# One gated DeltaNet layer on one Trainium2 core: a list scheduler in the source orders all five engines

## Chip, cores, metric

One NeuronCore of a Trainium2 chip. The metric is the device time of one execution in microseconds.

## What is computed

With DEPTH = 1 only the gated DeltaNet layer runs: T = 1024 tokens, D = 1024, 8 query/key heads and 16 value heads of width 128, chunks of 64 tokens in the reference. All of it is float32.

```python
hdn = rms_norm(x, norm_g) * (1 + scale) + shift          # shift, scale, gate from silu(c) @ ada_w
proj = hdn @ w_in                                        # q, k, v (convolved), z, b, a
qkv = silu(causal_depthwise_conv(qkv, conv_w))           # 4 taps
beta = sigmoid(b); g = -exp(a_log) * softplus(a + dt_bias); gc = cumsum(g) in a chunk
A = strict_lower(beta * k k^T * decay);  T = (I + A)^-1
# per chunk, with the state S carried on:
v_new = T (beta v) - T (beta k exp(gc)) S
o = q exp(gc) S + lower(q k^T decay) v_new
S = S exp(g_last) + (k exp(g_last - gc))^T v_new
y = (rms_norm(o) * silu(z)) @ w_out
out = rms_norm(x + gate * y)
```

## The kernel before

The kernel works in chunks of 128 tokens and in groups of two value heads that share one key/query head: 8 groups. Every float32 product of the projections is made of three float32r products (high and low parts of both sides), so one projection tile of 128 channels by 512 tokens is 24 matmuls of 512 columns (`project`, L453).

After a prologue (normalization, modulation, first projections) the main loop (L928) runs nine stages, gi = -1 to 7. In stage gi these generators run side by side:

- `scan` (L677) of group gi: per chunk three matmuls in turn, with VectorE's r (L739), vd (L758) and st (L771) between them, then the output, its norm and its gate z.
- `stage_a` (L534) of group gi+1: `norms` (L487) loads the decay table em from DRAM, exponentiates it, transposes k and q and takes their norms; then 8 products k k^T and q k^T, a store D1 of the diagonal 32x32 blocks and a load ua of them, 62 dependent VectorE operations on tm and tb (L575, L577: the solve), a store D2, and `levels` (L587), which loads TT and puts the 32x32 inverses together to 64 and 128 on TensorE.
- the filler: z projections (`out_gate`, L667), v projections (`values`, L632) of group gi+1, k/q projections (`proj_kq`, L474) of group gi+2. Each half tile of k, q or v goes through `Conv` (L430): two ScalarE copies out of PSUM, three VectorE operations, a SiLU.
- in stage 1 also `residual_gate` (L781).

`load_w` (L130) loads a projection weight tile in two halves (DMA, ScalarE cast, GpSimd subtraction). `early` (L861) begins the output product with the first four of 16 row blocks of w_out, for two time tiles of 512 tokens; it takes the memory of hdn and so can start only after the last projection. It loads w_out's two column halves in turn (`load_wo`, L805) and loads the first again for the second time tile, 12 loads in all.

Only TensorE's order is written out by hand there. `drive` (L902) keeps a clock of its own, `now`, that grows by a cost per matmul; a generator yields (cost, delay) and comes back no sooner than `delay` later. The delays are the constants D_... at L40 to L45, D_L0 = 46000 ns between the last product of `stage_a` and `levels` among them. In between filler matmuls are placed; in the last two stages also the units of `early` (tail), beside the NE = 15 units put into stage 6. The other four engines' instructions are put in order by the framework's scheduler.

After the loop, the other 12 row blocks of w_out follow (`load_wo2`, L814), then the residual, the final norm and the stores.

Of the kernel before, what the change touches and what calls it, by code (L numbers as in the profile page):

```python
# [35 lines left out]
TURN = 40  # L36
MM = 216

START, START1 = 11000, 65000
D_G, D_RG = 9500, 11000  # L40
D_N, D_A0, D_A = 3000, 1500, 1000
D_L0, D_L1, D_L2, D_L3 = 46000, 1600, 1800, 1600
D_R, D_V, D_S = 500, 1100, 700
D_F0, D_F = 8000, 2000
# [3 lines left out]
def gdn_layer(ctx: ExitStack, tc: tile.TileContext, x, c, ada_w, ada_b, norm_g, w_in, conv_w, a_log, dt_bias,  # L48
# [222 lines left out]
    def gates():  # L271

        w4 = lambda name: wpool.tile([P, 4, P], F32, name=name, tag="wraw", bufs=3)
        ba = [w4("ba").rearrange("p a b -> p (a b)") for _ in range(NHALF)]
        gt = w4("gt")
        yv, u, sv, s2 = [gt[:, i] for i in range(4)]
# [5 lines left out]
        pba = q0.tile([P, NT, 2 * HV], F32, name="pba", tag="xn", bufs=1)  # L282
        nc.scalar.copy(pba, ptb[:, :, 2 * HV:])
        nc.vector.tensor_tensor(pba, pba, ptb[:, :, :2 * HV], op=ALU.add)
        gt = w4("gt")
        q, g, grow, below = [gt[:, i] for i in range(4)]
        gh = w4("gh")[:, 0]
        nc.gpsimd.tensor_tensor(below, ones, triu, op=ALU.subtract)
        nc.vector.tensor_tensor(v3(yv), pba[:, :, HV:], dtb[:, None, :].to_broadcast(GS), op=ALU.add)
        nc.scalar.activation(u, yv, AF.Abs)  # L290
        nc.scalar.activation(u, u, AF.Exp, scale=-1.0)
        nc.scalar.activation(beta, pba[:, :, 0:HV], AF.Exp, scale=-1.0)

        nc.vector.tensor_scalar_add(sv, u, 2.0)
        nc.vector.reciprocal(sv, sv)
        nc.vector.tensor_tensor(sv, sv, u, op=ALU.mult)
        nc.vector.tensor_tensor(s2, sv, sv, op=ALU.mult)
        nc.vector.tensor_scalar_mul(q, s2, 1.0 / 17.0)
        for d in (15, 13, 11, 9, 7, 5, 3):
            nc.vector.scalar_tensor_tensor(q, q, 1.0 / d, s2, op0=ALU.add, op1=ALU.mult)  # L300
        nc.vector.scalar_tensor_tensor(q, q, 1.0, sv, op0=ALU.add, op1=ALU.mult)
        nc.vector.tensor_scalar_max(yv, yv, 0.0)
        nc.vector.scalar_tensor_tensor(yv, q, 2.0, yv, op0=ALU.mult, op1=ALU.add)
        nc.vector.scalar_tensor_tensor(v3(g), v3(yv), -1.0, nea[:, None, :].to_broadcast(GS), op0=ALU.mult,
                                       op1=ALU.mult)
        yield 0, D_G

        pgc = bank("ts", (P, 4, P))
        nc.vector.tensor_copy(gh.rearrange("p (h n) -> p n h", n=NT), v3(g))
# [4 lines left out]
        nc.scalar.copy(grow, pgc[:, 3])  # L314
        nc.sync.dma_start(out=gc_dram.rearrange("h n c -> (h n) c"), in_=grow)
        nc.vector.tensor_scalar_mul(ngc, v3(pgc[:, 0]), -1.0)
        nc.scalar.activation(eall, pgc[:, 0:3], AF.Exp)
        nc.vector.tensor_scalar_mul(negc, egc, -1.0)
        nc.vector.tensor_scalar_add(beta, beta, 1.0)
        nc.vector.reciprocal(beta, beta)  # L320
        yield 650, 0
# [94 lines left out]
    gate_steps = gates()  # L416
    with tc.manual_schedule(engines=GENG):
        next(gate_steps)
        drain(len(units))
# [9 lines left out]

    class Conv:  # L430
# [5 lines left out]
        def __call__(self, ps, dst, tag="xb", bufs=2):  # L436
            xb = cp.tile([P, TH + NTAP - 1], F32, name="xb", tag=tag, bufs=bufs)
            if self.prev is None:
                nc.gpsimd.memset(xb[:, 0:NTAP - 1], 0.0)  # L439
            else:  # L440
                nc.vector.tensor_copy(xb[:, 0:NTAP - 1], self.prev[:, TH:])
            nc.scalar.copy(xb[:, NTAP - 1:], ps)
            tp = taps[:, :, self.ct:self.ct + 1]
            nc.scalar.mul(dst, ps, tp[:, NTAP - 1])  # L444
            for j in range(NTAP - 1):
                nc.vector.scalar_tensor_tensor(dst, xb[:, j:j + TH], tp[:, j], dst, op0=ALU.mult, op1=ALU.add)  # L446
            nc.scalar.activation(dst, dst, AF.Silu)
            self.prev = xb
# [4 lines left out]
    def project(w, m, half):  # L453

        ps = bank("pj")
        hi, lo = w
        for k in range(KT):
            for n, (a, b) in enumerate(((hi, h_hi), (hi, h_lo), (lo, h_hi))):
                nc.tensor.matmul(ps[:m], lhsT=a[:, k, :m], rhs=b[half][k // 4][:, k % 4], start=(k == 0 and n == 0),  # L459
                                 stop=(k == KT - 1 and n == 2))  # L460
                yield MM
        return ps

    def trans():
        return bank("tr", (P, 4, P))

    kq0 = new_kq()
    for j, ct in ((0, 8), (1, 0)):
        cv = Conv(ct)
        for hf in range(NHALF):  # L470
            cv(acc0[j][hf], kq0[hf][:, j], tag="vtok", bufs=3)


    def proj_kq(gi, kq):  # L474
        for j, ct in ((0, 8 + gi), (1, gi)):
            w = load_w(ct * P, P, wpool)
            cv = Conv(ct)
            for hf in range(NHALF):
                if j == 0:
                    kq.append(cp.tile([P, 2, TH], F32, name="kq", tag="kq", bufs=4))  # L480
                ps = yield from project(w, P, hf)
                cv(ps, kq[hf][:, j])

    class Group:
        pass

    def norms(gi, G):  # L487

        kq, h0 = G.kq, 2 * gi
        G.em, G.ktok, G.rinv, G.oeps, G.brk, G.bkd, G.TT = [], [], [], [], [], [], []  # L490

        em = cp.tile([P, 2, NT, P], F32, name="em", tag="em", bufs=2)
        nc.sync.dma_start(out=em.rearrange("p h n c -> p (h n c)"),
                          in_=gc_dram[h0:h0 + 2].rearrange("h n c -> (h n c)")[None, :].to_broadcast([P, 2 * T]))
        for n in range(NT):
            for h in range(2):
                nc.vector.scalar_tensor_tensor(em[:, h, n], em[:, h, n], ngc[:, n, h0 + h:h0 + h + 1], mask,  # L497
                                               op0=ALU.add, op1=ALU.add)
        nc.scalar.activation(em, em, AF.Exp)
        for hf in range(NHALF):  # L500
            n0 = 4 * hf

            ssk = cp.tile([P, 4], F32, name="ssk", tag="ssk")
            ssq = cp.tile([P, 4], F32, name="ssq", tag="ssq")
            ktok = cp.tile([P, 4, P], F32, name="ktok", tag="ktok", bufs=4)
            pk = trans()
            for j in range(4):
                nc.tensor.transpose(pk[:, j], kq[hf][:, 0, j * P:(j + 1) * P], ident)
            yield 430, 0
            nc.scalar.copy(ktok, pk)  # L510
            for j in range(4):
                nc.scalar.activation(pk[:, j], pk[:, j], AF.Square, accum_out=ssk[:, j:j + 1])
            pq = trans()
            for j in range(4):
# [19 lines left out]
    def stage_a(gi, G):  # L534

        kq, ats = G.kq, []
        if not hasattr(G, "bkd"):
            yield from norms(gi, G)
# [497 lines left out]
```

## Time and profile before

| | us |
|---|---|
| median of 3 runs | 1133.0 (1131.27 to 1133.68) |
| the profiled execution | 1130.95 |
| its span, first to last instruction | 1129.2 |
| TensorE's mean granted clock | 0.979 of 2.4 GHz |

The rows below come from the page of the profiled execution and from questions to its trace. Engines: PE is TensorE, PEld its weight loads, DVE VectorE, ACT ScalarE, POOL GpSimd, SP the queue that issues DMAs. A group row has line, engine, operation, output<-inputs, shapes and count, then the busy time in us and the mean of one in ns, then the idle time ahead of them and what ended it. A row of stretches has the stretch, its length, per engine the busy time and count, the granted TensorE clock, the share of time the DMA engines worked, GB/s. A row of the time line has start, duration, engine, line, operation. A matmul's duration overlaps the next one's, so the rate of matmuls is read from the distance of their starts.

### The profile page before, as it was taken

The numbers are of one execution on the slowest core, as the hardware profiler recorded it, in microseconds if no ns is written. First come the engines' busy times: TensorE is split into PE (matmuls) and PEld (weight loads), VectorE is DVE, ScalarE is ACT, GpSimd is POOL, SyncE is SP. The second block draws the span as 40 slices with busy tenths as digits, with TensorE's granted clock in tenths as the row PEclk, the third lists the DMA queues.
The fourth block names the chain that finished last, engine by engine and source line by source line (L and its number), as shares of the span: only waits on it lengthen the run. The fifth ranks groups of instructions, "written<-read, shape, count | busy, mean of one in ns | idle before, by whom it ended". The sixth has DMA issues, their size and how long they took to land.

```text
span 1129.2 us, 18338 instructions
## 1 busy us (share of the span) xinstructions
PE 1059.3 (94%) x6295; PEld 857.6 (76%) x6295; DVE 745.1 (66%) x1914; ACT 536.6 (48%) x1416; POOL 450.0 (40%) x532
## 2 busy tenths in 40 slices
PE   8997999989999799999999999999899989999997
PEld 7875787767878678777877887788678768778785
DVE  5468775776579857865786677677766866513515
ACT  6567442453642455435543644364546424534523
POOL 3452223532444135323532452155216334954643
PEclk9998999999999999999999999999999989999999
DMA  9803333341145313421531143125313571446442
GB/s 287 234 19 133 75 82 85 101 126 43 39 135 164 83 50 100 125 56 30 145 102 45 42 146 84 39 54 163 74 29 103 149 219 63 140 135 185 152 121 75
DMA packets 188131, 119.48 MB, mean 106 GB/s; under 512 B 59733, under 2 KB 166534, under 8 KB 187014
## 3 DMA queue, kind: packets, MB, share of 16 engines
q1 hardware_dynamic: 187536, 118.20, 37.2%
q8 instruction: 50, 0.82, 0.3%
q14 instruction: 43, 0.35, 0.1%
q10 hardware_dynamic: 502, 0.10, 0.0%
HBM read 93.03 MB, written 25.24 MB: 105 GB/s over the span
## 4 chain that ended last, share of the span: by engine, by line
PE 41%; DVE 18%; ACT 6%; POOL 5%; DMA 4%; issue 4%; SPq 0%; POOLq 0%; DVEq 0%; ACTq 0%
PE pj L459 16%; PE pj L837 5%; DVE tb L577 4%; DVE tm L575 4%; DVE vT L446 3%; DVE em L497 3%; PE tr L549 2%; PE tr L837 2%; PE ts L755 2%; PE ks L736 1%; PE oq L709 1%; PE oq L762 1%; PE tr L622 1%; PE ks L767 1%; PE tr L628 1%
## 5 line engine op out<-in xcount | busy, mean ns | idle before, releaser
L124 POOL TENSOR_TENSOR wlo<-wraw,whi 128x512 fp32r<-128x512 f32 x92 | 126.1, 1379 | 147.3 <-ACT whi L123 107.7
L446 DVE SCALAR_TENSOR_TENSOR vT<-xb,taps,vT 128x512 f32<-128x512 f32 x96 | 84.6, 882 | 24.3 <-ACT vT L444 23.3
L446 DVE SCALAR_TENSOR_TENSOR kq<-xb,taps,kq 128x512 f32<-128x512 f32 x96 | 78.7, 828 | 12.9 <-ACT kq L444 11.0
L123 ACT CAST whi<-wraw 128x512 fp32r<-128x512 f32 x92 | 55.5, 618 | 64.9 <-PE pj L459 59.0
L577 DVE TENSOR_TENSOR tb<-tb,tm 128x126 f32<-128x126 f32 (+22 forms) x248 | 80.1, 323 | 4.8
L698 POOL TENSOR_TENSOR oT<-oT,z 128x256 f32<-128x256 f32 x64 | 50.6, 792 | 81.2 <-ACT oT L697 74.0
L575 DVE TENSOR_TENSOR tm<-tb,ua 128x126 f32<-128x126 f32 (+22 forms) x248 | 78.3, 316 | 6.2 <-DMA ua<-D 1.1
L459 PE MATMUL pj<-h1hia,whi 128*128 128x512 f32 x184 | 75.8, 412 | 6.6 <-ACT vT L444 6.6
L697 ACT ACTIVATE oT<-pot,cols 128x256 f32<-128x256 f32 x64 | 30.4, 474 | 108.1 <-PE pot L695 54.8
L459 PE MATMUL pj<-h0lob,whi 128*128 128x512 f32 x184 | 78.2, 425 | 0.0
L459 PE MATMUL pj<-h0hia,whi 128*128 128x512 f32 x184 | 76.8, 417 | 1.3 <-ACT kq L444 1.3
L459 PE MATMUL pj<-h1hib,whi 128*128 128x512 f32 x184 | 77.8, 423 | 0.0
L459 PE MATMUL pj<-h1lob,whi 128*128 128x512 f32 x184 | 77.7, 422 | 0.0
L459 PE MATMUL pj<-h1hia,wlo 128*128 128x512 f32 x184 | 77.5, 421 | 0.0
L459 PE MATMUL pj<-h0hib,wlo 128*128 128x512 f32 x184 | 77.1, 419 | 0.0
L459 PE MATMUL pj<-h1hib,wlo 128*128 128x512 f32 x184 | 76.6, 416 | 0.0
L459 PE MATMUL pj<-h0hia,wlo 128*128 128x512 f32 x184 | 75.8, 412 | 0.0
L459 PE MATMUL pj<-h1loa,whi 128*128 128x512 f32 x184 | 75.7, 411 | 0.0
L459 PE MATMUL pj<-h0loa,whi 128*128 128x512 f32 x184 | 75.6, 411 | 0.0
L459 PE MATMUL pj<-h0hib,whi 128*128 128x512 f32 x184 | 75.5, 410 | 0.0
L439 POOL MEMSET xb<- 128x3 f32 x32 | 3.4, 109 | 172.3 <-DVE kq L446 85.9
L719 POOL TENSOR_TENSOR sso<-sso,neg_half 128x2 f32<-128x2 f32 x64 | 44.6, 696 | 58.3 <-DVE sso L718 57.6
(445 smaller groups left out, 2933.1 us busy)
## 6 DMA issues: line engine op xcount, KB each, us to landing
wraw<-in_gdn_w_in SPq DMA_DIRECT2D x92, 256.0 KB, 2.9
woraw<-in_gdn_w_out SPq DMA_DIRECT2D x54, 256.0 KB, 3.2
wa<-in_ada_w SPq DMA_DIRECT2D x16, 512.0 KB, 6.9
em<-gc_dram SPq DMA_DIRECT2D x8, 1024.0 KB, 6.4
z_dram<-sz SPq DMA_DIRECT2D x32, 256.0 KB, 2.1
z<-z_dram SPq DMA_DIRECT2D x64, 128.0 KB, 2.4
o_dram<-oT SPq DMA_DIRECT2D x64, 128.0 KB, 1.9
gsrc<-o_dram SPq DMA_DIRECT2D x32, 256.0 KB, 2.9
```

The lines of the kernel that those rows point to most:

```text
L123: nc.scalar.copy(hi, raw)
L124: nc.gpsimd.tensor_tensor(lo, raw, hi.bitcast(F32), op=ALU.subtract)
L446: nc.vector.scalar_tensor_tensor(dst, xb[:, j:j + TH], tp[:, j], dst, op0=ALU.mult, op1=ALU.add)
L459: nc.tensor.matmul(ps[:m], lhsT=a[:, k, :m], rhs=b[half][k // 4][:, k % 4], start=(k == 0 and n == 0), stop=(k == KT - 1 and n == 2))
L497: nc.vector.scalar_tensor_tensor(em[:, h, n], em[:, h, n], ngc[:, n, h0 + h:h0 + h + 1], mask, op0=ALU.add, op1=ALU.add)
L549: nc.tensor.matmul(pg2[:, 0:2], lhsT=kq[hf][:, 0, js], rhs=kq[hf][:, :, js], start=True, stop=True)
L575: nc.vector.tensor_tensor(tmv, tb[:, :mm, j:j + 1].to_broadcast([P, mm, ln]), ua[:, j:j + 1, j + 1:].to_broadcast([P, mm, ln]), op=ALU.mult)
L577: nc.vector.tensor_tensor(tb[:, :mm, j + 1:], tb[:, :mm, j + 1:], tmv, op=ALU.subtract)
L697: nc.scalar.mul(oT, pot, normw_c)
L698: nc.gpsimd.tensor_tensor(oT, oT, zs.pop(n), op=ALU.mult)
L719: nc.gpsimd.tensor_tensor(sso, sso, neg_half[:, :2], op=ALU.pow)
L837: nc.tensor.matmul(acc, lhsT=a[:, ts], rhs=b, start=(first and n == 0), stop=(last and n == 2))
```

## The change

A class `Order` in the source keeps a model of four queues (ScalarE, VectorE, GpSimd, SP) with a price for each operation. A generator no longer issues an instruction of these engines itself: it puts it into a queue as an `Op` with its price, the operations it must come after and a rank. `advance` takes, as the model's clock reaches them, the operation that can start first, among those of one time the lowest rank, and issues it. A step of TensorE yields a condition (inputs done in the model plus LATP) and is issued at the first moment at which it holds; `drive` asks the streams in a fixed order, the filler last. The whole region is fixed for all five engines. A `loader` runs as a generator of its own through the list of all projection weight tiles. Gates, norms, convolutions, the solve, the levels and the scan compute what they did. `early_loads` keeps both column halves of the first four row blocks of w_out (one in the memory of hdn, one in the projection weights' buffers), so 8 loads. The units of `early` in stage 6 are those that `take` gives; the rest runs in the last stage.

```diff
-TURN = 40
-MM = 216
-START, START1 = 11000, 65000
-D_G, D_RG = 9500, 11000
-D_L0, D_L1, D_L2, D_L3 = 46000, 1600, 1800, 1600
...
+MM, M4, M2, TP = 231, 430, 218, 436
+LAT, LATP, DMA = 150, 250, 2800
+TABLE = 1283
+AC = {512: 530, 256: 400, 128: 240}
+VC = {512: 690, 256: 340, 128: 265}
...
+    def advance(self, upto):
+        while True:
+            best = None
+            for eng, q in self.queue.items():
+                if not q:
+                    continue
+                free = self.free.get(eng, 0)
+                ready = [(max(t, free), op) for op in q[:80] if (t := op.start()) is not None]
+                if not ready:
+                    continue
+                t = min(r[0] for r in ready)
+                op = min((r for r in ready if r[0] <= t), key=lambda r: r[1].rank)[1]
+                if best is None or t < best[0]:
+                    best = (t, eng, op)
+            if best is None or best[0] > upto:
+                return
+            t, eng, op = best
+            self.queue[eng].remove(op)
+            op.fn()
+            if op.table and op.table != self.table:
+                t, self.table = t + TABLE, op.table
+            op.end = t + op.cost
...
+    def loader():
+        while True:
+            yield lambda: bool(wq) and order.avail("w", 2)
+            c0 = wq.pop(0)
...
+                d = load(lambda raw=raw, ks=ks, c0=c0: nc.sync.dma_start(out=raw, in_=wv[:, ks, c0:c0 + P]))
+                a = act(lambda raw=raw, ks=ks, hi=hi: nc.scalar.copy(hi[:, ks], raw), 512, d, rank=2)
+                ops.append(pool(lambda raw=raw, ks=ks, hi=hi, lo=lo: nc.gpsimd.tensor_tensor(
+                    lo[:, ks], raw, hi[:, ks].bitcast(F32), op=ALU.subtract), 1290, a, holds=r))
...
     def norms(gi, G):
...
+        yield lambda: hasattr(order, "gate") and done(*order.gate, order.gc)
+        d = load(lambda: nc.sync.dma_start(
+            out=em.rearrange("p h n c -> p (h n c)"),
...
+        d = order.put("sp", 2500, lambda: None, (d,))
+        e = [vec(lambda n=n, h=h: nc.vector.scalar_tensor_tensor(
+            em[:, h, n], em[:, h, n], ngc[:, n, h0 + h:h0 + h + 1], mask, op0=ALU.add, op1=ALU.add), 128, d, rank=2)
+             for n in range(NT) for h in range(2)]
+        G.emop = act(lambda: nc.scalar.activation(em, em, AF.Exp), 1820, *e, table="exp")
...
     def gates(ptb, held):
+        gt = cp.tile([P, 8, P], F32, name="gt", tag="at", bufs=2)
...
     def stage_a(gi, G, old):
...
+            d = [vec(lambda j=j, mm=mm, ln=ln, tmv=tmv: nc.vector.tensor_tensor(
+                tmv, tb[:, :mm, j:j + 1].to_broadcast([P, mm, ln]), ua[:, j:j + 1, j + 1:].to_broadcast([P, mm, ln]),
+                op=ALU.mult), 170 + mm * ln * 3 // 4, *d, rank=2)]
...
-        yield 0, D_L0
-        yield from levels(gi, G, 0)
+        yield from levels(gi, G, 0, old)
...
     def scan(gi, G):
...
+                ro = [vec(lambda h=h, n=n, pks=pks, r=r, vtok=vtok, j=j: nc.vector.scalar_tensor_tensor(
+                    r[:, h], pks[:, 0, h], negc[:, n, h0 + h:h0 + h + 1], vtok[:, j, h], op0=ALU.mult, op1=ALU.add), 128,
+                          rank=-1) for h in range(2)]
...
+    def early_loads():
+        yield lambda: not order.projecting
...
+            if tg == 0:
+                wset[0] = wos[:EARLY]
+                for i in range(EARLY // 2):
+                    hi, lo = [wpool.tile([P, 2, TH], F32R, name=n, tag=t, bufs=2)
+                              for n, t in (("wohi", "whi"), ("wolo", "wlo"))]
+                    wset[1] += [(hi[:, n], lo[:, n]) for n in range(2)]
...
+            for kt in range(EARLY):
+                yield lambda: order.avail("sz", 2)
+                g(kt, tg)
...
+    def drive(runs, must):
+        idle = 0
+        while not all(r.over for r in must):
+            order.advance(order.now)
+            if any(r.step() for r in runs):
+                idle = 0
             else:
+                order.now += 50
...
-    with tc.manual_schedule(engines={nc.tensor.engine}):
+    with tc.manual_schedule(engines=ORDERED(nc)):
...
+                    more = itertools.chain(done_projecting(), take(tail, NE))
...
+            drive(background + must + ([trun] if gi == HQ - 1 else []), must)
+        drive(background + [trun], [trun])
+        order.flush()
```

## Rows read from the trace of the kernel before

**Rows 1.** The page, section 1: busy us, share of the span, instructions.
```profile
PE 1059.3 (94%) x6295; PEld 857.6 (76%) x6295; DVE 745.1 (66%) x1914; ACT 536.6 (48%) x1416; POOL 450.0 (40%) x532
```

**Rows 2.** Busy time by stretch: stages A, G0, G1, G3, G5, G6, G7, O.
```profile
77.20:183.65 106.45, 98.34 (x537) 78.22 (x537) 80.80 (x219) 56.62 (x135) 29.11 (x35) 0.95 0.35 97
183.65:296.15 112.50, 106.58 (x698) 86.01 (x699) 77.13 (x195) 45.96 (x115) 35.52 (x48) 0.97 0.29 77
296.15:411.34 115.19, 105.96 (x668) 85.81 (x667) 92.30 (x274) 53.51 (x153) 40.48 (x51) 0.99 0.39 106
...
520.46:628.71 108.25, 103.49 (x651) 83.56 (x650) 75.75 (x203) 52.97 (x152) 40.21 (x51) 0.98 0.31 81
...
735.20:841.72 106.52, 101.78 (x651) 82.48 (x650) 75.63 (x203) 53.05 (x152) 39.71 (x51) 1.00 0.31 82
841.72:939.19 97.47, 89.84 (x539) 72.38 (x537) 72.06 (x189) 45.21 (x143) 43.10 (x49) 0.96 0.50 148
939.19:990.00 50.81, 49.12 (x301) 40.55 (x302) 28.77 (x63) 26.63 (x86) 38.06 (x44) 1.00 0.32 98
990.00:1129.20 139.20, 129.00 (x559) 104.06 (x557) 48.96 (x69) 52.46 (x103) 68.99 (x56) 0.99 0.43 135
```

**Rows 3.** Time line of PE: projection matmuls at two moments.
```profile
98.77 0.63 PE L459 MATMUL pj<-h0hib,whi 128*128 128x512 f32 x1
99.20 0.63 PE L459 MATMUL pj<-h0lob,whi 128*128 128x512 f32 x1
...
586.62 0.40 PE L459 MATMUL pj<-h1loa,whi 128*128 128x512 f32 x1
586.85 0.40 PE L459 MATMUL pj<-h1hia,wlo 128*128 128x512 f32 x1
```

**Rows 4.** Waits of PE in G3 (520 to 628): us in total, times, longest.
```profile
PE pj L459 <- ACT vT L444: 1.7, 1, 1.7
PE tr L639 <- ACT vT L447: 0.9, 1, 0.9
PE tr L613 <- ACT pn L609: 0.8, 1, 0.8
PE tr L614 <- DVE pn L610: 0.7, 1, 0.7
PE tr L508 <- ACT tr L512: 0.7, 1, 0.7
```

**Rows 5.** The page, section 6: DMA issues, KB each, median us to landing.
```profile
woraw<-in_gdn_w_out SPq DMA_DIRECT2D x54, 256.0 KB, 3.2
em<-gc_dram SPq DMA_DIRECT2D x8, 1024.0 KB, 6.4
...
ua<-D SPq DMA_DIRECT2D x16, 256.0 KB, 4.1
```

**Rows 6.** Groups of VectorE instructions over the whole span.
```profile
L446 DVE SCALAR_TENSOR_TENSOR kq<-xb,taps,kq 128x512 f32<-128x512 f32 x96 | 78.7, 828 | 12.9 <-ACT kq L444 11.0
...
L497 DVE SCALAR_TENSOR_TENSOR em<-em,ngc,mask 128x128 f32<-128x128 f32 x128 | 50.0, 409 | 1.0 <-DMA em<-gc_dram 1.0
```

**Rows 7.** Waits of PE in G6 and G7 (841 to 990).
```profile
PE pj L837 <- ACT h0hia L810: 3.4, 2, 2.6
PE pj L837 <- DVE h0hib L811: 2.4, 2, 2.1
PE pj L837 <- POOL h0hib L811: 1.0, 1, 1.0
```

**Rows 8.** G6 again, output products (L837) alone: PE, PEld, clock, DMA.
```profile
841.72:939.19 97.47, 27.68 (x96) 18.94 (x96) 0.96 0.50 148
```

**Rows 9.** Time line of DVE and POOL near 567 us.
```profile
566.72 0.30 DVE L575 TENSOR_TENSOR tm<-tb,ua 128x136 f32<-128x136 f32 x1
567.05 1.35 DVE L577 TENSOR_TENSOR tb<-tb,tm 128x136 f32<-128x136 f32 x1
...
566.95 2.60 POOL L124 TENSOR_TENSOR wlo<-wraw,whi 128x512 fp32r<-128x512 f32 x2 [1.41 <-ACT whi L123]
```

More of the change, by code (lines that the diff above doesn't have):

```diff
@@ L457, in project @@
+    def project(c0, half, last):
+        yield lambda: c0 in wready and done(*wready[c0][1]) and free("pj")
+        (hi, lo), _, held = wready[c0]
+        ps, ph = bank("pj"), order.hold("pj", 1 if c0 >= Z0 else 2)
         for k in range(KT):
             for n, (a, b) in enumerate(((hi, h_hi), (hi, h_lo), (lo, h_hi))):
-                nc.tensor.matmul(ps[:m], lhsT=a[:, k, :m], rhs=b[half][k // 4][:, k % 4], start=(k == 0 and n == 0),
+                nc.tensor.matmul(ps, lhsT=a[:, k], rhs=b[half][k // 4][:, k % 4], start=(k == 0 and n == 0),
@@ L460, in project @@
                                  stop=(k == KT - 1 and n == 2))
[L461 to L474, printed above, removed]
+                order.now += MM
+                if k < KT - 1 or n < 2:
+                    yield None
+        if last:
+            held.append(order.mark())
@@ L479, in proj_kq @@
                 if j == 0:
[L480 to L485, printed above, removed]
+                    G.kq.append(cp.tile([P, 2, TH], F32, name="kq", tag="kq", bufs=4))
+                ps, ph = yield from project(ct * P, hf, hf == NHALF - 1)
+                G.kqop[hf][j] = cv(ps, ph, G.kq[hf][:, j], [old.passed[hf]] if old else [])
+                yield None
@@ new lines, in values @@
+        waiting = []
+        source = itertools.chain(tiles(), more or [])
+        end = object()
+        y = next(source, end)
+        while y is not end:
+            if ready():
+                turn(*waiting.pop(0)[1:])
+                yield None
+            elif y is None:
+                yield None
+                y = next(source, end)
+            else:
+                yield lambda: y() or ready()
+                if y():
+                    y = next(source, end)
+        while waiting:
+            yield ready
+            turn(*waiting.pop(0)[1:])
+            yield None
@@ new lines, in gdn_layer @@
+    order.projecting, order.early0 = True, False
+    Gs = [Group(gi) for gi in range(HQ)]
+    zgates = [out_gate(head, Gs[head // 2]) for head in range(HV)]
+    zheads = list(range(HV))
+    background = [Run(loader()), Run(early_loads())]
+    tail = early()
+    trun = Run(tail)
+    rows = []
+    for gi in range(-1, HQ):
+        heads, zheads = zheads[:ZQ[gi + 1]], zheads[ZQ[gi + 1]:]
+        tiles = [16 + 2 * (gi + 1) + h for h in range(2)] if gi + 1 < HQ else []
+        pair = [8 + gi + 2, gi + 2] if gi + 2 < HQ else []
+        zc = [Z0 + h * P for h in heads]
+        wq += ([c * P for c in pair + tiles] + zc) if gi < 0 else zc + [c * P for c in tiles + pair]
```

731 lines of the change are left out of this document (452 added, 279 removed).

## The prediction

> **What bounds the kernel now.** I read the page's line of busy shares first: TensorE is busy for 94% of the span, no other engine for more than 66% [rows 1]. So a change that keeps every matmul can win only what TensorE does not use. To see where that is, the second view cuts the span into stages: a lead-in from the first projection to the first scan (77.20 to 183.65), then one stage per head group, each beginning with the first matmul of its scan, then the output tail from 990 [rows 2]. I call them A, G0 to G7 and O. In each row the reader takes span minus TensorE's busy time, and the granted clock. Idle: A 8.1, G0 5.9, G1 9.2, G2 5.2 and G3 4.8 (one row stands for both), G4 and G5 4.7 each (likewise), G6 7.6, G7 1.7, O 10.2 us. The clock has two levels, so a mean of 0.95 over 106.45 us stands for a tenth of it at 1.2 GHz, and half of that tenth is lost: 0.05 x 106.45 = 5.3 us in A, likewise 3.4 in G0, 1.2 in G1, 2.2 in G2, 2.2 in G3, nothing in G4 and G5, 3.9 in G6. That such stretches exist is seen in matmul starts: 0.43 us apart after the idle time ahead of 98 us, 0.23 us apart elsewhere [rows 3]. Idle plus half-rate loss is 42.6 + 14.3 = 57.0 us in A to G5 and 13.2 in G6 and G7.
>
> Third, who ends the idle time. One ordinary stage, G3, has five waits: 1.7 us for a PSUM bank that ScalarE had not emptied, 0.9 for a SiLU ahead of a transposition, 0.8 and 0.7 in the block inverse, 0.7 for squares, 4.8 in all [rows 4]. No wait for projection weights is among them. So weights do not bound the steady stages, and a stream of their own cannot win there by itself. VectorE's 75.75 us in G3's 108.25 leave it room on average [rows 2].
>
> **The change, part by part.** The sum is made against the profiled execution, 1130.95 us (its span is 1129.2); the median of the three runs is 2.05 us above it.
>
> *Order of TensorE.* Before, a step was placed a fixed delay after the step it depends on; now it is placed when the scheduler's own model says that its inputs are finished plus 0.25 us, and projection matmuls go in wherever nothing else is ready. A perfect model would take all 57.0 us of A to G5: the matmuls themselves are the same, and G5 shows that with 4.7 us of idle time the clock stays at its upper level, so with less idle time none of the 14.3 us need remain. That is one end.
>
> The other end is what the model's prices leave out. Its prices stand in the code, the chip's in rows. The em load: 2.8 + 2.5 = 5.3 in the model, 6.4 in the row [rows 5], late by 1.1. The sixteen em operations: 0.265 against 0.409 [rows 6], 16 x 0.144 = 2.3. The 24 convolution operations of a stage: 0.69 against 0.828, 24 x 0.138 = 3.3. The ua load: 2.8 against 4.1, 1.3. Together 8.0 us per stage. Because all five queues are now fixed, a late load stands at the head of its queue: behind VectorE's first em operation wait the scan's r, vd and st, and TensorE's next scan matmul for those. But VectorE has 30% of the stage free to catch up, so between 0 and 8.0 us per stage reach TensorE. I take 3.0: the nearest row is today's 4.8 of waits in G3 [rows 4], which come from the same kind of mismatch, less the 1.7 of the bank wait, where a readiness rule puts another matmul. Seven stages, A to G5: 21 us of new waits, bounds 0 to 56. Net -57.0 + 21 = -36.
>
> *Five fixed queues.* The issue of every DMA is now in a fixed order on SP, which the model gives no issue time. Weight loads, z, o, D1, ua, D2 and TT all pass through it. What this costs is in the loads' lateness above. On ScalarE the model adds 1.283 us per table change but prefers by rank; em's Exp still stands among SiLUs, so it costs two changes a stage as before. That is nothing on TensorE's path, as ScalarE is busy 52.97 of 108.25 us in G3 [rows 2]; without that cover it is 2.6 per extra pair.
>
> *Gates.* Their elementwise chain moves behind the lead-in's last matmuls, into memory of the next pool. No row shows when that memory is free; the nearest is A's idle time, 8.1 us [rows 2], so 0 to 8.1. I take 1, near the lower end, since A has 336 projection matmuls to put in front; without them the chain's lateness counts whole.
>
> *Weights stream.* The same 92 loads, casts and subtractions; only their place changes. 0, hidden by two tile sets; an uncovered set would cost a load, a cast and a subtraction, but no row shows TensorE waiting for one.
>
> *Early output weights.* Both halves of the first four are kept, so the second time tile begins without four more loads, four casts and four subtractions. In rows, that is the longest of the waits for h0hia, 2.6, and the 1.0 for POOL's h0hib [rows 7], 3.6 us. Against it, their loads now start only after the last projection matmul, where before only cast and subtraction were late (2.1 for VectorE's h0hib and the other 0.8 for h0hia). A weight load is 3.2 [rows 5], and four g tiles go through two buffers; 0 to 5, I take 3. Net -0.6. The resident half also occupies the weight buffers that the next output weights want, until halfway through the second time tile; its other half is four accumulators of twelve matmuls, 48 x 0.23 = 11 us, which covers a 3.2 us load, so 0, and the 3.2 if the load falls behind them.
>
> *Filler in G6.* Before, output products filled G6 whenever nothing else was ready: 96 matmuls, 32 units of three [rows 8]. Now `take` ends after 15 units there; the rest waits for G7. The 17 units x 3 x 0.23 = 11.7 us are not lost work, but if group 7's inverse is still unfinished, TensorE idles for that long. With only three projection tiles in that stage VectorE's solve runs faster, so 0 to 11.7; I take 4.
>
> Sum: -36 + 1 - 0.6 + 4 = -31.6, so 1130.95 - 31.6 = 1099.4 on the profiled execution and 1101 for the median.
>
> **The rivals.** *Late queues (slower).* If all 8.0 us per stage reach TensorE, A to G5 pay 56 against 57 won; with the 11.7 of G6, 1.4 of handover (5 against 3.6) and 1 for the gates that is +13, 1144, or 1146 for the median. It decides from (57.0 - 11.7 - 1.4 - 1)/7 = 6.1 us of new waits per stage. For it speaks that a list rule places each dependent matmul with almost no slack, where the old delay before the inverse was generous; against it VectorE's free time.
>
> VectorE's prices are also for an idle GpSimd: a tb operation beside two weight subtractions took 1.35 us, the one before it 0.30 [rows 9]. The new order does not know this, but neither did the old one know it better, so it stays within the 8.0. The Trainium skill, "SBUF — State Buffer", section "Who interferes with whom", says that a VectorE instruction with two SBUF inputs and a GpSimd instruction that reads SBUF exclude each other for a whole instruction. The row agrees. By that rule alone each of the twelve subtractions of a stage could hold one priority operation for about a microsecond, which would carry this rival past its point; no row says that the new order meets more of them than the old.
>
> *All idle time goes.* New waits near 0: -57.0, G6's 3.9 of half rate and the 3.6 of weights go too, with nothing of the 1, 3 and 4 above, 1130.95 - 64.5 = 1066.5, 1068 for the median. For it: each of G3's waits is one that a readiness rule can fill with a projection matmul. Against it: the inverse chain of a stage (em, solve, two loads, two inverses) has latencies that no order removes.
>
> *It moves nothing.* New waits equal to the old, about 1133: needs 6 us a stage by accident.
>
> **How the numbers follow.** Forecast with 2 to 5 us of new waits a stage: 0.43. All goes: 0.25. Late queues: 0.27. Nothing: 0.05. The range reaches from the second case, 1066, into the third, 1145, leaving about one in ten at each side. A change under 0.2% could not be told from none. Faster 0.68, same 0.05, slower 0.27. The forecast's own range, 2 us a stage and no idle time in G6 up to 5 and all 11.7, is 1090 to 1123.
>
> **What would show it.** Right: stages of 101 to 105 us in place of 106 to 109, a clock of 1.00 in G2 and G3, the waits of rows 4 gone and shorter ones for r, vd, st or TE in their place. G6 shorter than 97.5, G7 longer than 51. Wrong: waits of over 6.1 us in a stage, VectorE idle for a DMA while TensorE waits for VectorE; or a stage that ends with TensorE idle before the next scan because the inverse ended last. The forecast also falls if A, whose chain from gates to first scan is long, grows.

## The result and the profile after

The changed kernel took 1213.6 us (median of 4 runs, 1209.8 to 1215.7) where the kernel before took 1132.9 on the same chip (4 runs): 1.071 times as long, 95% interval 1.068 to 1.074. The prediction was 1101, with a range of 1066 to 1145. It had the wrong sign and missed by 112.6 us.

The profiled execution has a span of 1213.9. First the page's busy line, the answer to [rows 1]: as many matmuls (x6295), VectorE and ScalarE busy for some 6 us more each, and a longer span. Of the 84.7 us that the span grew by, 30.7 are TensorE's busy time (1059.3 before) and 54.0 its idle time: the same matmuls also ran more slowly.

```profile
PE 1090.0 (90%) x6295; PEld 870.9 (72%) x6295; DVE 752.1 (62%) x1913; ACT 542.3 (45%) x1415; POOL 436.0 (36%) x530
```

Then the stretches of [rows 2], cut in the same way at the first scan matmul of each group: A, G0, G1, G3, G5, G6, and what follows to the end in two pieces. The columns are those of [rows 2].

```profile
80.05:202.79 122.74, 100.55 (x510) 79.74 (x511) 83.33 (x219) 60.87 (x142) 26.82 (x32) 0.89 0.23 66
202.79:313.02 110.23, 105.58 (x726) 84.69 (x725) 72.71 (x180) 42.56 (x112) 34.11 (x47) 0.98 0.31 84
313.02:450.12 137.10, 110.53 (x668) 88.07 (x667) 96.73 (x286) 56.69 (x157) 42.32 (x53) 0.91 0.30 82
...
560.25:671.52 111.27, 104.91 (x651) 83.25 (x650) 77.42 (x203) 53.41 (x152) 38.12 (x51) 0.98 0.29 79
...
783.52:896.21 112.69, 105.81 (x652) 83.99 (x651) 77.42 (x203) 53.42 (x152) 38.12 (x51) 0.97 0.29 78
896.21:1010.20 113.99, 87.89 (x463) 68.85 (x461) 74.30 (x197) 49.96 (x145) 37.93 (x49) 0.86 0.36 109
1010.20:1062.00 51.80, 49.91 (x324) 39.97 (x323) 29.01 (x65) 24.42 (x82) 32.89 (x41) 0.98 0.33 107
1062.00:1213.90 151.90, 141.89 (x614) 114.41 (x612) 51.52 (x73) 52.73 (x103) 76.76 (x61) 0.99 0.40 128
```

Against before: lead-in +2.9, A +16.3, G0 -2.3, G1 +21.9, G2 to G5 +1.0, +3.0, +5.5 and +6.2, G6 +16.5, the rest +13.7. That is the whole 84.7. Three stages stand out by their clock (0.89, 0.91, 0.86) and by span minus TensorE's busy time: A 22.2, G1 26.6 and G6 26.1 us, where before had 8.1, 9.2 and 7.6. Matmuls have moved too: 27 fewer in A and 28 more in G0, 76 fewer in G6 and 78 more behind it. So G6 lost more than its length says, and the tail, which grew by 13.7, lost nothing: 78 matmuls at 0.23 us are 18 us.

Who ends TensorE's idle time, over the whole span (us in total, times, longest). In these lines `tr`, `pot`, `ks` and `pj` are PSUM banks, `TE` holds the blocks from which `levels` builds the inverse, `oT` is a chunk's output on its way to DRAM, `accg` the sums of the residual gate, `vT` a v tile after its convolution, and `h0hia` and its like are parts of hdn's memory that now hold output weights.

```profile
PE tr L766 <- DVE TE L758: 24.5, 2, 15.0
PE pot L892 <- ACT oT L896: 20.0, 6, 4.9
PE tr L1020 <- DVE accg L1016: 17.8, 4, 7.6
PE ks L982 <- DVE vd L967: 6.2, 10, 2.6
PE pj L1066 <- ACT h0hia L1121: 4.7, 3, 2.3
```

The first line is the inverse's start at the end of A (15.0) and of G6 (9.6). The third is the residual gate at the end of G1. The second comes about once a stage: ScalarE, which empties the bank `pot`, cannot go on until a buffer oT is free. In G3 it is nearly all that is left. Of the five waits of [rows 4] four have gone, as forecast; the second, 0.9 us for a SiLU ahead of a transposition, stands there unchanged (now L813):

```profile
PE pot L892 <- ACT oT L896: 4.4, 1, 4.4
PE tr L813 <- ACT vT L561: 0.9, 1, 0.9
PE ks L940 <- DVE st L987: 0.3, 1, 0.3
```

The durations of [rows 5] and [rows 6] hardly moved, or fell (em's load from 6.4 to 5.3), so the loss is not in these operations. DMA issues, then two VectorE groups:

```profile
woraw<-in_gdn_w_out SPq DMA_DIRECT2D x50, 256.0 KB, 3.0
em<-gc_dram SPq DMA_DIRECT2D x8, 1024.0 KB, 5.3
```

```profile
L557 DVE SCALAR_TENSOR_TENSOR kq<-xb,taps,kq 128x512 f32<-128x512 f32 x96 | 78.3, 825 | 30.4 <-ACT kq L554 23.5 <-POOL xb L547 5.0
L641 DVE SCALAR_TENSOR_TENSOR em<-em,ngc,mask 128x128 f32<-128x128 f32 x128 | 46.0, 405 | 0.0
```

What did move is the place of em. One stage of each kernel, 628.7 to 735.2 before and 671.5 to 783.5 after (start, duration): the em operations on VectorE, the Exp on ScalarE, the first product k k^T on TensorE. Before, one of sixteen em operations stands for all:

```profile
678.52 0.34 DVE L497 SCALAR_TENSOR_TENSOR em<-em,ngc,mask 128x128 f32<-128x128 f32 x1
...
691.18 1.91 ACT L499 ACTIVATE em<-em 128x2048 f32<-128x2048 f32 x1
...
640.68 0.60 PE L549 MATMUL tr<-kq 128*128 128x256 f32 x2
```

After:

```profile
659.59 0.46 SPq L637 DMA_DIRECT2D em<-gc_dram  x1
...
677.74 0.32 DVE L641 SCALAR_TENSOR_TENSOR em<-em,ngc,mask 128x128 f32<-128x128 f32 x1
...
690.48 1.92 ACT L644 ACTIVATE em<-em 128x2048 f32<-128x2048 f32 x1
...
693.01 1.03 PE L704 MATMUL tr<-kq 128*128 128x256 f32 x4
```

Before, the product stands 12.0 us into the stage, and the em operations at 50 us are those of the *next* stage's group: the framework's scheduler had moved them a stage ahead, to where the scan lets go of em's buffer. After, em's operations run at 6 to 19 us into the stage that needs it, and the product follows at 21.5. The load is not what holds them: it was issued at 659.6, and the page's median to landing is 5.3 us. They stand in VectorE's fixed order among the next stage's operations.

### The profile page after: what moved, and what is told of

Same layout as the page of the kernel before. It is cut to its first block, busy times and chain, and to the rows that moved or that the text cites. A ratio compares the mean times of both kernels' runs of the same rounds, so it can differ in the third digit from the quotient of the medians.

```text
span 1213.9 us, 18304 instructions
## 1 busy us (share of the span) xinstructions
PE 1090.0 (90%) x6295; PEld 870.9 (72%) x6295; DVE 752.1 (62%) x1913; ACT 542.3 (45%) x1415; POOL 436.0 (36%) x530
## 4 chain that ended last, share of the span: by engine, by line
PE 46%; DVE 18%; ACT 15%; DMA 8%; issue 6%; POOL 5%; SPq 2%; DVEq 0%; POOLq 0%; ACTq 0%
PE pj L598 24%; PE pj L1066 3%; DVE tm L733 2%; DVE vT L557 2%; DVE tb L736 2%; DMA woraw<-in_gdn_w_out 2%; DVE kq L557 2%; DVE em L641 2%; PE tr L797 2%; POOL wolo L206 2%; PE tr L789 2%; ACT tr L669 2%; DMA o_dram<-oT 2%; ACT tr L662 1%; ACT junk L918 1%
## 5 line engine op out<-in xcount | busy, mean ns | idle before, releaser
L587 POOL TENSOR_TENSOR wlo<-wraw,whi 128x512 fp32r<-128x512 f32 x88 | 116.2, 1336 | 317.1 <-ACT whi L586 305.0
L733 DVE TENSOR_TENSOR tm<-tb,ua 128x126 f32<-128x126 f32 (+22 forms) x248 | 88.7, 358 | 52.7 <-DMA ua<-D 46.4
L557 DVE SCALAR_TENSOR_TENSOR vT<-xb,taps,vT 128x512 f32<-128x512 f32 x96 | 78.3, 816 | 20.0 <-ACT vT L554 19.0
L736 DVE TENSOR_TENSOR tb<-tb,tm 128x126 f32<-128x126 f32 (+22 forms) x248 | 83.8, 338 | 7.1
L552 ACT COPY xb<-pj 128x512 f32<-128x512 f32 x62 | 36.3, 585 | 101.1 <-PE pj L598 97.4
L598 PE MATMUL pj<-h0hib,whi 128*128 128x512 f32 x184 | 78.4, 426 | 0.0
L922 POOL TENSOR_TENSOR sso<-sso,neg_half 128x2 f32<-128x2 f32 x64 | 45.0, 705 | 84.9 <-DVE sso L920 76.1
L951 POOL TENSOR_TENSOR sg<-st,eall 128x256 f32<-128x256 f32 x48 | 30.2, 629 | 103.8 <-ACT st L985 103.8
L206 POOL TENSOR_TENSOR wolo<-woraw,wohi 128x512 fp32r<-128x512 f32 x36 | 48.1, 1356 | 46.8 <-ACT wohi L205 46.8
L897 POOL TENSOR_TENSOR oT<-oT,z 128x256 f32<-128x256 f32 x64 | 47.7, 746 | 45.1 <-ACT oT L896 44.1
```

What stands on the lines that cost most here:

```text
L206: nc.gpsimd.tensor_tensor(lo, raw, hi.bitcast(F32), op=ALU.subtract)
L552: a = act(lambda: nc.scalar.copy(xb[:, NTAP - 1:], ps), 512, *old, rank=0, holds=held)
L557: d = [vec(lambda j=j: nc.vector.scalar_tensor_tensor(dst, xb[:, j:j + TH], tp[:, j], dst, op0=ALU.mult, op1=ALU.add), 512, *d)]
L587: ops.append(pool(lambda raw=raw, ks=ks, hi=hi, lo=lo: nc.gpsimd.tensor_tensor(lo[:, ks], raw, hi[:, ks].bitcast(F32), op=ALU.subtract), 1 ...
L598: nc.tensor.matmul(ps, lhsT=a[:, k], rhs=b[half][k // 4][:, k % 4], start=(k == 0 and n == 0), stop=(k == KT - 1 and n == 2))
L733: d = [vec(lambda j=j, mm=mm, ln=ln, tmv=tmv: nc.vector.tensor_tensor(tmv, tb[:, :mm, j:j + 1].to_broadcast([P, mm, ln]), ua[:, j:j + 1, j ...
```

## The experiments

Each version ran once, except c4, c4_pe_only, c3_timed and the two c5 (four runs each). One run is good to some 5 us: the first projection, behind a lead-in that no kernel here changes, began between 76.1 and 81.0 us; the same kernel c3 took 1153.3 and, on another chip, 1148.3; and the kernel before took 1139.2 beside e1a, e2, e3 and e6_peonly, 1133.2 beside e1f, e4m, e5w and c1, and 1133.6 beside h_em, g_two_stages, c2 and c3. A total therefore counts with the stage lengths beside it.

**e1a: the residual gate, last in line and due a stage later.**

```diff
-                streams.append(residual_gate())
+                rg = Run(residual_gate())
...
-            drive(background + must + ([trun] if gi == HQ - 1 else []), must)
+            if gi == RG + 1:
+                must.append(rg)
+            drive(background + must + ([rg] if gi == RG else []) + ([trun] if gi == HQ - 1 else []), must)
```

> Theory (stage ends): the 7% is lost mostly at three stage ends where a chain off TensorE ends last and TensorE has no filler left: A (gates to first inverse), G1 (residual gate), G6 (inverse, with the filler cut at 15 units). In this kernel the residual gate starts in stage 1 as before, is served last, and must be done only by the end of stage 2. Expected: G1 falls from 137 to 114 to 119, G2 to G5 stay at 110 to 113, total 1190 to 1197 (from 1213.6). Rival (late queues): underpriced operations in five fixed queues delay TensorE everywhere; the gate's 72 operations then only move their delay into stage 2: G1 at least 125 or G2 at least 122, total 1206 to 1216.

1254.5 us, slower, and neither as forecast: behind a filler that is nearly always ready the gate got no turn in G1, and ran whole at the end of G2. G1 and G2, then TensorE's waits over the span:

```profile
309.81:421.69 111.88, 105.52 (x651) 83.82 (x650) 77.44 (x203) 53.27 (x152) 38.21 (x51) 0.97 0.29 79
421.69:603.13 181.44, 111.17 (x669) 88.10 (x667) 102.00 (x286) 56.05 (x157) 41.07 (x53) 0.80 0.24 64
```

```profile
PE tr L1020 <- DVE accg L1016: 63.8, 8, 10.9
```

The miss measures the chain: without it G1 is 111.9, so it costs G1 25 us, and one slice (two loads through one buffer, nine operations, a matmul) takes 8 us with nothing else to do.

**e2: NE from 15 to 32.**

> Only NE is changed, from 15 to 32: stage 6 gets all units of the first time tile as filler. Stage ends: the 10 us hole before group 7's inverse and the half-rate stretches around it are filled with 17 units of three matmuls (11.7 us); G6 stays near 114 with more work in it and G7 with the tail falls by about 12, total 1199 to 1205. Late queues: G6 is as long as its late queues make it and the units themselves wait for their loads there; G6 grows by 6 to 12, total 1210 to 1216.

1206.5 us, 1.5 above the first theory's range. G6 stayed at 114.1 with 508 matmuls in place of 463, as it had it, but what follows fell by 6.7 us (203.7 to 197.0) and not by 12. About 7 us.

**e3: the gates first, em of group 0 ahead.** Ranks only.

```diff
-        V = lambda fn, *after, cost=330: order.put("dve", cost, fn, after, rank=0)
-        A = lambda fn, *after: order.put("act", 350, fn, after, table="exp")
+        V = lambda fn, *after, cost=330: order.put("dve", cost, fn, after, rank=-2)
+        A = lambda fn, *after: order.put("act", 350, fn, after, rank=-2, table="exp")
...
-            em[:, h, n], em[:, h, n], ngc[:, n, h0 + h:h0 + h + 1], mask, op0=ALU.add, op1=ALU.add), 128, d, rank=2)
+            em[:, h, n], em[:, h, n], ngc[:, n, h0 + h:h0 + h + 1], mask, op0=ALU.add, op1=ALU.add), 128, d, rank=2 if gi else -1)
```

> Only ranks are changed: the gates' ScalarE and VectorE operations get rank -2 (ahead of the first convolutions and casts) and the em operations of group 0 rank -1 in place of 2. Stage ends: A falls from 122.7 to 107 to 114 because its chain (gates, em, products, ua, solve, D2, TT) begins 5 to 10 us earlier; total 1199 to 1208. Late queues: the convolutions that are pushed back delay the first projections' banks and the norms instead, A stays at 120 to 125, total 1210 to 1216.

1201.3 us. A fell from 122.7 to 110.8, as the first theory had it: the gates' matmuls begin at 99.8 us in place of 110.5 (before: 87.6).

**e6_peonly: four engines freed.** `ORDERED = lambda nc: {nc.tensor.engine}`

> Only ORDERED is changed: TensorE's order stays the new one, the other four engines are ordered by the framework's scheduler as in the kernel before. Stage ends: TensorE's order and filler keep the holes (G1 at least 128, G6 at least 108); total 1195 to 1225. Late queues: with four free queues the waits go; steady stages G2 to G5 fall from 110 to 113 to below 108, G1 below 122, total below 1170.

1220.8 us, level with the changed kernel if one allows for a chip on which the kernel before took 1139.2: G1 136.8, G3 to G5 112.3 to 112.6. Level is a sum of two opposite moves: A is 11.4 longer (134.1) and G6 11.2 shorter (102.8, where at least 108 was expected). The framework put em back at 46 to 72 us of the stage before, yet G2 to G5 did not shorten; the reading that fits is that TensorE's order had been planned round a late em. In G4 the oT wait had gone and 5.4 us of waits for vT stood in its place.

**e1f: the gate's rank from 3 to 0.**

> Only the rank of the residual gate's VectorE operations is changed, from 3 (last) to 0. e1a showed G1 at 111.9 when the gate is not asked for in it, so the gate costs G1 25 us. Stage ends, with the rank as the reason: the eight slices are done before the inverse, G1 falls to 112 to 118, total 1188 to 1196. Rival: the 8.1 us of one slice (two loads in one buffer, nine operations) are the reason and not the rank: the last slices still end last, G1 stays above 125, total above 1202.

1212.8 us, G1 133.3, as the rival had it: the rank is worth at most the 3.8 us by which G1 fell, so the serial slices remain.

**e4m: the scheduler told of the two oT buffers.** The output transposition is held back until the store of the buffer before last, priced at 4.5 us, has landed in the model.

```diff
+            kept = order.hold("oT", 1)
...
-            load(lambda: nc.sync.dma_start(
-                out=o_dram[h0:h0 + 2, :, n * P:(n + 1) * P].rearrange("h e t -> e h t"), in_=oT), b)
+            order.put("sp", 4500, lambda: nc.sync.dma_start(
+                out=o_dram[h0:h0 + 2, :, n * P:(n + 1) * P].rearrange("h e t -> e h t"), in_=oT), (b,), holds=kept)
...
-            return late and late[0][0] in zs and done(late[0][2]) and free("pot")
+            return late and late[0][0] in zs and done(late[0][2]) and free("pot") and order.avail("oT", 2)
```

> The scheduler is told what it did not know: there are two oT buffers, and one comes free only when its store has landed (4.5 us). A chunk's output transposition is then held back, and other matmuls go in, where before TensorE waited 2 to 4.9 us for the bank pot in each of five stages. Stage ends and holes: that wait goes, G2 to G5 fall from 110 to 113 to 105 to 108, because the half-rate stretch behind the hole goes with it; total 1188 to 1198. Late queues: TensorE waits for the same lateness elsewhere, stages stay at 110 or more, total 1207 to 1216.

1212.4 us; G4 109.8 (112.0). In G4 the wait for pot is 0.3 in place of 4.2, and another has taken its place:

```profile
PE tr L813 <- ACT vT L561: 3.6, 1, 3.6
```

That wait was 0.9 in the changed kernel. In the same stretch VectorE waits at the head of its queue for a load of the solve (6.7 in the changed kernel):

```profile
DVE tm L733 <- DMA ua<-D: 8.5, 1, 8.5
```

So the rival is right that curing one end moved the wait to another. That the late load makes the vT wait is not shown: the load's wait ends 17 us before the vT wait does.

**e5w: VectorE's prices as measured.** `VC = {512: 830, 256: 410, 128: 320}`

> Only the model's VectorE prices are changed to those measured before: 0.83 for 512 columns, 0.41 for 256, 0.32 for 128 (from 0.69, 0.34, 0.265). Late queues by mis-priced VectorE operations: steady stages fall by 3 us each or more, total below 1195. Stage ends and holes: the prices are not what makes them; total 1203 to 1222.

1214.8 us, G3 to G5 112.1 to 112.4. In G4 the wait for pot had gone, and others of 6.5 us in all stood there; no stage from G2 to G5 became shorter by more than 0.6. VectorE's prices are not what makes the loss. The prices of the em and ua loads, 2.4 of the forecast's 8.0 us, were not tried.

**c1: four edits together** (e3, e1f, e4m, NE 30).

> The four edits together: NE 30, the ranks of the gates and of em, the rank of the residual gate, and the two oT buffers told to the scheduler. If the loss is the four named holes, the gains add up: about 14 + 16 + 24 + 20, total 1130 to 1148, near the kernel before. Late queues: the holes come up elsewhere, total above 1165.

1181.9 us, by its total where the rival had it (above 1165). By stage it is neither: A (110.2) and the NE 30 part gained as before (195.1 behind G6 in place of 203.7), but G1 stayed at 131.9 and G2 to G5 at 110 to 111.5.

**h_em: em put in ahead.** The load, the sixteen operations and the Exp of `norms` become a step of their own.

```diff
+    def decay_ahead(gi, G, old):
+
+        yield lambda: hasattr(old, "scanned")
+        decay(gi, G)
+        yield None
...
                 streams.append(scan(gi, Gs[gi]))
+                if gi + 2 < HQ:
+                    streams.append(decay_ahead(gi + 2, Gs[gi + 2], Gs[gi]))
```

> One step is moved: the decay table em of group gi+2 (its load, sixteen VectorE operations and the Exp) is put into the queues as soon as the scan of group gi has ended, in the stage before the one that needs it, where the kernel before has it (44 to 63 us into a stage). In the changed kernel its operations run 6 to 18 us into the stage that needs it and the products k k^T begin at 21 to 22 us instead of 12. Theory (a chain that starts late): G2 to G5 fall from 110 to 113 to 103 to 108, G6's hole of 9.6 us halves, total 1175 to 1192. Rival (late queues whatever the chain): TensorE's waits for oT, vT and TE stay, G2 to G5 at 109 or more, total 1200 to 1216.

1192.4 us, 0.4 above the range of the theory and below the rival's. G2, G3, G5, G6:

```profile
453.54:563.93 110.39, 105.78 (x651) 84.35 (x651) 73.07 (x200) 51.06 (x148) 36.04 (x49) 0.97 0.31 83
563.93:670.56 106.63, 102.87 (x651) 82.09 (x650) 77.28 (x203) 52.81 (x152) 38.90 (x51) 1.00 0.31 82
...
777.90:884.33 106.43, 102.91 (x651) 82.09 (x650) 77.31 (x203) 52.82 (x152) 39.15 (x51) 1.00 0.30 82
884.33:987.75 103.42, 87.76 (x459) 67.48 (x458) 65.41 (x180) 45.02 (x142) 37.30 (x48) 0.87 0.41 120
```

G3 to G5 are back at 106.4 to 107.3 with a clock of 1.00 (106.5 in G4 and G5 of the kernel before), and G6 is 10.6 shorter, with 5.8 us of waiting for TE in place of 9.6. G2 stayed at 110.4; in c3 below, where the gate also leaves G1, it is 106.3. In G4 the product begins 9.6 us into the stage, and the wait for oT is gone without a word about oT buffers. Raising em's rank in every group, without moving it, was not tried. Of G4's waits these two are left above 0.3 us:

```profile
PE ks L954 <- DVE st L1001: 2.0, 1, 2.0
PE tr L827 <- ACT vT L561: 1.8, 2, 1.5
```

**g_two_stages: the gate in stages 0 and 1**, ahead of the filler, due at the end of stage 1.

> The residual gate starts in stage 0, served ahead of the filler, and has to be done by the end of stage 1. The eight serial slices of 8 us then lie in two stages. If its chain is what stretches G1: G1 falls from 137 to 110 to 114 (111.9 in the run in which the gate was not asked for there) and G0 grows by at most 4; total 1186 to 1196. If the time is lost to VectorE's load and not to the chain: G0 and G1 together stay above 240, total above 1205.

1194.8 us, as expected: G0 and G1 together 225.3 (247.3). The chain's place was the cost.

```profile
201.64:315.11 113.47, 108.06 (x739) 86.56 (x738) 87.23 (x249) 42.09 (x112) 34.05 (x47) 0.97 0.38 101
315.11:426.91 111.80, 105.67 (x656) 84.09 (x655) 79.39 (x214) 53.73 (x153) 38.29 (x51) 0.98 0.33 92
```

**c2 and c3: all of it, with and without the oT buffers.** Gate in two stages, e3, NE 30, em ahead; c2 also e4m.

> Five edits: NE 30, ranks of the gates and of em of group 0, the gate in two stages, the two oT buffers told to the scheduler, and em put in ahead. If the named causes are additive: A 110, G0 110, G1 110, G2 to G5 104 to 106 each, G6 104, tail about 200, total 1118 to 1145: level with the kernel before or below it. If late queues take the place of each hole: total above 1155.

> As the run before, without the two oT buffers told to the scheduler. If the oT wait of 4 us a stage still comes, 1 to 5 us a stage more than the run before, 1125 to 1160; if it has gone with the earlier chain, equal within 4 us.

c2 took 1166.4, which is above 1155, where the rival had it; c3 1153.3. In c3 the gains add up: 12.3 (e3), 7.1 (e2), 21.2 (h_em) and 18.8 us (g_two_stages) from 1213.6 make 1154.2. The kernel before is not reached. That the two differ by 13 us fits neither case of c3's expectation: e4m's edit now costs 13 us. In c3 TensorE waits nowhere for oT; in c2, with the edit that was to prevent it, it does:

```profile
PE pot L907 <- ACT oT L911: 12.1, 5, 3.2
```

Why the edit brings that wait back was not tried.

**h_em_pe_only, c4 and c4_pe_only.** c4 spreads the gate's slices over stages 1 to 4; the other two free four engines.

> As h_em (em put in ahead), and only TensorE's order is fixed; the other four engines are ordered by the framework. With em late, freeing the four engines changed nothing (1220.8 where the kernel before took 1139.2). If the late em in TensorE's order is what made the steady stages long, and the fixed queues as such cost little: G2 to G5 105 to 109, total 1183 to 1200, level with h_em (1192.4). If fixed queues cost by themselves and were only covered by the late chain: G2 to G5 below 104, total below 1178.

> As c3 (1153.3), with the residual gate spread over stages 1 to 4, two to three slices in each, in place of stages 0 and 1. c3's G0 of 117.7 carries some 70 of the gate's operations on VectorE and its inverse ends late. Expected: G0 110 to 113, G1 to G4 107 to 110, total 1144 to 1154. If the gate costs the same wherever it is: within 2 us of c3.

> As c4, and only TensorE's order is fixed. If the fixed queues are worth something: 3 to 20 us slower than c4, since the framework's order puts SiLUs and casts where TensorE's planned order does not have them (h_em_pe_only's and e6's waits for vT). If they cost something: 3 to 20 us faster, and then level with the kernel before.

h_em_pe_only took 1192.0, level with h_em, and again as a sum of opposite moves: A is 11.4 longer than in h_em (7.4 with its lead-in) and G2 4.0, G1 7.5 shorter and G6 5.3. c4: 1158.5, 1.0225 times the kernel before (1.0178 to 1.0272), neither as expected nor within 2 us of c3: G0 fell to 109.5, but G2 grew to 113.9, and G0 to G4 together are 551.4 (546.3 in c3). Spread over four stages the gate costs some 5 us more. c4_pe_only: 1153.7, 1.0177 (1.0134 to 1.0219). Four freed engines gave 4.8 us, but not the level of the kernel before that was expected with it.

**c3 timed, c5_x_later, c5_pe_only.** c5 puts the loads of the x rows behind the first output weights.

> c3 again, timed in the same call as the two below: 1150 to 1160. The edits in it: em put in ahead, the gate in two stages, the ranks in A, NE 30.

> As c3, and the four loads of x rows for the first time tile (2 MB) are put in behind the first set of output weights and o, not together with them. In c3 at 910 to 935 us the DMA engines are busy 85 to 101% and TensorE 15 of 25 us: waits for h0hia 4.6, h0hib 2.0, h0lob 0.8 and TE 4.6. If the loads compete at this handover: these waits halve, total 4 to 8 us below c3_timed. If the weights' loads, casts and subtractions are late by themselves because they begin only after the last projection: the same within 2 us.

> As c5_x_later with only TensorE's order fixed. c4 against c4_pe_only showed 4.8 us for free engines; expected 2 to 8 us below c5_x_later. If the fixed queues gain at the handover: above it.

c3: 1148.3 us, 1.0132 (1.0105 to 1.0160). c5_x_later: 1152.1, 1.0154 (1.0116 to 1.0193), as neither forecast had it, 3.8 above c3. The waits for h0hia, h0hib and h0lob at the handover came to 6.7 us, against 6.1 in the c3 timed beside it: moving the x rows away did not shorten them, so competition with those rows is not what makes them. That they come from a late start of the weights' own loads is left, and not shown by itself. c5_pe_only: 1146.7, 1.0111 (1.0084 to 1.0139), 5.4 below c5 and the lowest of all; these handover waits are absent from it, and its G6 is 103.4 where c3's is 109.1, though this wait has come in their place:

```profile
PE tr L827 <- ACT vT L561: 9.4, 3, 5.6
```

The two pairs agree on some 5 us for free engines, though in each the two intervals overlap. No version beat the kernel before.

## Why the prediction was wrong, point by point

**Order of TensorE (-36 forecast).** This step failed: in place of the 36 us that A to G5 were to give back, they grew by 51.6. The step let the term run between two ends: a perfect model takes all of the 57.0 us in A to G5, and only what the model's prices leave out comes back. Both ends assume that the plan itself has no holes there. It has, and they can be counted in the plan, ahead of any run: `drive` adds 50 ns to its clock whenever no stream can go on, and these steps add up, per stage, to

```
stage                     A     G0   G1    G2..G5   G6
changed kernel, us idle   19.9  0    22.1  0        19.4
c3, us idle               10.3  0    0     0         8.9
```

These are the scheduler's own numbers, no times of the chip; but they name the three stages in which the chip's rows show 22, 27 and 26 us of idle time. Idle plus half-rate loss in A to G5, by the forecast's own reckoning, became 78.0 + 38.1 = 116.1 us in place of 57.0. (That reckoning is generous on both sides: it takes the clock's share of a whole stage, idle time included, where a low clock costs nothing.) A list rule places what is ready. It does not start a long chain early for the sake of what hangs on its end, and where all filler has gone before the chain's end, TensorE stands still. "G5 shows that with 4.7 us of idle time the clock stays at its upper level" was right, and worked the other way: behind the longer holes the granted clock fell (0.89 in A, 0.91 in G1).

**New waits of 3.0 us a stage from prices (bounds 0 to 8.0).** In size this was inside its bounds, at nearly twice the value taken: in G4 TensorE's waits are 5.6 us, and the stage is 5.5 longer than before. The cause was another, so it is luck that the bounds held the waits. With measured VectorE prices (e5w) G4 stayed at 112.4; with em ahead (h_em) it was 107.3. That the waits sit where VectorE is held by ua and stores of oT land late (up to 4.6 us in that stage, 2.3 before) is seen; that em's delay brings these two together is argued from it, not shown alone.

**Five fixed queues ("what this costs is in the loads' lateness").** This missed what fixing takes away. The rows had it: [rows 6] show em's load ending only 1.0 us of VectorE's idle time, and a timeline would have shown em a stage ahead of its use. I priced em's operations and never asked in which stage they stood. Worth 15.6 us in G3 to G5 and 10.6 in G6 by h_em. Fixed queues as such: about 5 us in total by c4 and c5 and 0 by h_em and e6_peonly, where fixing them made A 7 to 11 us shorter and G6 5 to 11 us longer.

**Gates (+1, bounds 0 to 8.1).** A grew by 16.3 with 27 matmuls fewer. "Near the lower end, since A has 336 projection matmuls to put in front" failed: TensorE had nothing left to run for the last 15.0 us ahead of the inverse. The gates' matmuls were 23 us later than before, half of it cured by ranks (e3).

**The residual gate.** It is no term of the sum at all, though `streams.append(residual_gate())` stood in both kernels. Before, the framework had loaded and begun its first slice by 79.5 us and the sums of its slices end no wait of TensorE; after, the stage could not end without it: G1 grew by 22 us.

**Weights stream (0).** Right: no wait for projection weights in either kernel.

**Early output weights (-0.6).** The waits at the handover, answering [rows 7], are 8.0 us against 6.8:

```profile
PE pj L1066 <- ACT h0hia L1121: 4.7, 3, 2.3
PE pj L1066 <- POOL h0hib L1122: 2.4, 2, 1.3
...
PE pj L1066 <- DVE h0lob L1113: 0.9, 1, 0.9
```

So the late loads are there, and the net is near zero with the other sign. c5_x_later speaks against "competing" with the x rows.

**Filler in G6 (+4, bounds 0 to 11.7).** Right mechanism, inside its bounds, and taken too small: in G6 51 output matmuls stand in place of the 96 of [rows 8], and TensorE waits 9.6 us for the inverse.

```profile
896.21:1010.20 113.99, 18.90 (x51) 12.17 (x51) 0.86 0.36 109
```

With 32 units (e2) about 7 us came back; of the rest of G6, 10.6 us hung on em's place (h_em).

**The rivals.** Late queues, 1146, had the sign, and e4m shows a wait that moves on when one end is cured, as that rival had it; but its place, 8 us in every stage, holds at most 16 of the 84.7 us, in G2 to G5, and em's place takes those too (h_em). The signs listed under "Wrong" came true by name: the inverse ending last, and a longer A. They should have been a rival of their own with a price: [rows 2] show TensorE idle for only 8 us of A, but not how many matmuls are left when the inverse starts.

What remains between c3 (timed) and the kernel before is, by stage: G6 +11.6, G0 +6.1, the tail +5.6, A with its lead-in +3.4, the others -9.3. Part of this is work that moved: A has 27 matmuls fewer than before and G0 40 more, G6 38 fewer and the tail 37 more (8.5 us at 0.23), so the tail is not long for its work. A and G6 are. Of G6 the handover (6.1 us) and 5.0 us for TE are seen; the rest stays open.

## What to carry to other kernels

Before an order is frozen on more engines, list what the old scheduler had moved ahead across stages; freezing takes it back, and here freeing the engines again did not bring it back while TensorE's order was planned around the late step (e6_peonly). A list scheduler that counts time counts its own idle time: print it by stage before reading any trace. A serial chain that must end with a stage has to start early in the plan; raising its rank took 3.8 us off its stage (e1f), starting it a stage earlier took 22.0 off G0 and G1 together (g_two_stages).

## What the runs showed of the hardware that was not expected

The clock after the hole in G6 of the changed kernel (the same columns as [rows 2], pieces of 5 to 10 us; the inverse starts at 998.3 after 9.6 us without a matmul):

```profile
990.00:995.00 5.00, 0.00 (x0) 0.00 (x0) 2.37 (x6) 0.00 (x0) 1.26 (x1) 0.70 0.45 96
995.00:1000.00 5.00, 0.92 (x26) 0.82 (x28) 1.30 (x3) 0.00 (x0) 0.00 (x0) 0.50 0.37 60
1000.00:1010.20 10.20, 8.37 (x85) 7.08 (x81) 3.08 (x6) 0.97 (x2) 0.20 (x1) 0.50 0.17 45
1010.20:1015.00 4.80, 4.80 (x19) 3.80 (x17) 2.13 (x5) 1.11 (x3) 1.07 (x1) 0.76 0.02 3
1015.00:1020.00 5.00, 5.00 (x96) 4.29 (x95) 3.40 (x10) 2.56 (x10) 2.17 (x3) 1.00 0.00 0
```

The granted clock was 0.50 (1.2 GHz) all through the inverse that followed, though TensorE was busy for 8.4 of 10.2 us. From 1010.2 to 1015.0 it was 0.76, and from 1015.0 to 1020.0, with TensorE busy without a gap, 1.00. Over the span TensorE was idle for 54.0 us more than before and busy for 30.7 us more with the same 6295 matmuls: by these two sums, an estimate, a hole cost about half as much again as it was long.
